# Attention heads' wide float32 products as three one-pass products of exact halves, and sums over partitions as two

## The chip, the cores and the metric

The kernel runs on one core of a Trainium2 chip. The metric is the device time of one execution in microseconds; the time before is the median of three runs. The engines are named as in the profile: PE multiplies (PEld is its weight load, which overlaps it), DVE is the vector engine, ACT the scalar (activation) engine, POOL the general one, SP the engine that issues most DMAs.

## What is computed

A two-layer decoder trunk on 256 tokens of width 2048, all in float32. Cut to the parts that the change touches:

```python
def memory_attention(q_m, mem, g_mem, w_mem_kv):        # both layers, 4 heads of 128
    s = jnp.einsum('bshd,bmhd->bhsm', q, k) * (MEM_HEAD_DIM ** -0.5)
    p = jax.nn.softmax(s, axis=-1)
    return jnp.einsum('bhsm,bmhd->bshd', p, v)

def mla_attention(...):                                 # layer 1, 12 heads, causal
    s = (einsum(q_nope, k_nope) + einsum(q_rope, k_rope)) * scale     # k_rope: one for all heads
    p = jax.nn.softmax(where(k_pos <= q_pos, s, -inf), axis=-1)
    return p @ v

def rmsnorm(x, g):
    return x * lax.rsqrt(jnp.mean(x * x, axis=-1) + EPS) * g
```

Layer 0 mixes with a gated unit beside the memory heads, layer 1 with the 12 causal heads beside the memory heads; each layer then has an output projection and a gated FFN of width 5632 with a short convolution.

## The kernel before

**Numbers.** The activations lie with features on the partitions and the 256 tokens in the columns. A large product is not done as a float32 product. Both operands are split into a high part of type fp32r (ACT copies the value to that type) and a low part, the exact rest (DVE subtracts). Then three products are added in PSUM: high by high, high by low, low by high. The big multiplications do this with weights `whi`, `wlo` and activations such as `xhl`, whose first 256 columns are the high part and whose last 256 are the low part (`mm_fm`, lines 148 to 155, and `mm_tm`, lines 181 to 186). The smaller products of the heads are plain float32 products: the memory heads' scores (line 584) and outputs (line 619), the causal heads' scores (line 956 for the plain part, line 957 for the rotary part) and outputs (lines 990 and 991), the sums over partitions by a matrix of ones (line 265), and all transposes by the identity. In the trace a plain float32 product shows as two instructions, an fp32r product as one.

**Weight stream.** `chunk` (line 95) loads a piece of weights (usually 128x1024) into `raw` (4 buffers), ACT writes `whi` (line 113; 5 buffers), DVE writes `wlo` (line 114; 5 buffers), and PE uses the two for 24 fp32r products of 256 columns, or 12 of 512. `whi` of a chunk is free again when the chunk's last product with it has run.

**Order.** The program text gives each instruction a priority. The order on every engine is fixed when the program is built, by a planner that runs a model of the engines' times (`schedule_with_timeline_sim=True`, line 1133) and gives each engine, at each moment of the model, the ready instruction that comes first in the text. On the chip every engine runs its list in that order, and an instruction that waits holds up all behind it on its engine. Dependencies and semaphores are added by the same layer. `hooks` are pieces of work that a big multiplication calls after the chunk of the given number.

**Stages.** The memory's keys `kT` and values `mv` for both layers, and the turned input `xhl`, come first (`start`). `layer_a` then does the gate's values, the memory queries `qm`, and the gate's other half in three multiplications; in the first two of these lie two memory heads each: scores after chunks 2 and 3, transposes after chunk 5, outputs after chunks 6 and 7. The spatial weights `wT` and biases `bb` are last used by `gates(9)` after chunk 0. `w_out`, `ffn`, `layer_b`, `w_out` and `ffn` follow.

**The heads of layer 1.** `layer_b` builds the latents (`latent`, with `rstd_bc`), the rotary key `krz` (line 894), the memory queries, and the values `v` (line 909) in `scratch`, which takes the place of `xhl`. Then a loop of six iterations, one for each pair of heads, does in iteration i:

- `queries(i)` and `keys(i)`: weights of three chunks, results copied by ACT into `qn` and `kn`;
- `rotary(i)`: six POOL instructions turn the pair's rotary queries into `qr`;
- `turn` of the pair before last and of a memory head: transposes of the probabilities, copied by ACT into `pT`;
- `scores` of the last pair: for each head, four products into one PSUM bank (128 and 256 keys; plain, then rotary), then mask and maximum (DVE, line 963), exponent (ACT, line 969), division (DVE, line 974);
- `attend` of the pair before last, `memory_out` of one memory head, `memory_scores` of the next.

After the loop stand `scores` of the last pair and `w_out`, which begins with the four memory heads' blocks and has the last two pairs' transposes and outputs as hooks. All of PSUM is eight banks, one tile each (`psum`).

`rstd_bc` (line 263) is called five times: for each FFN (after chunk 3 of its first multiplication), at the start of `layer_b`, and for the two latents. It multiplies the ones by `ssum`, a running sum of squares that POOL keeps (lines 271 to 275).

Of the kernel before, what the change touches and what calls it, by code (L numbers as in the profile page):

```python
# [16 lines left out]
P = 128  # L17
D = 2048
S = 256
# [50 lines left out]
class Kernel:  # L70
# [192 lines left out]
    def rstd_bc(self, out, ssum, n):  # L263
        acc = self.psum()
        self.nc.tensor.matmul(acc[:, :S], self.ones, ssum, start=True, stop=True)
        self.rstd(out, acc[:, :S], n, self.cp, "rb")
# [11 lines left out]
    def constants(self):  # L278
        nc, cp = self.nc, self.cp
        self.ident = cp.tile([P, P], F32, name="ident")  # L280
        make_identity(nc, self.ident)
        self.ones = cp.tile([P, P], F32, name="ones")
        nc.vector.memset(self.ones, 1.0)
        self.gT = cp.tile([P, 148], F32, name="gT")
        self.cT = cp.tile([P, 2, 4, FB * 2], F32, name="cT")
        self.g = {}
        self.ng = 0
# [142 lines left out]
    def start(self):  # L430
        nc, t, tc = self.nc, self.t, self.tc
        self.x = self.ap.tile([P, NB, S], F32, name="xT")
        self.xhl = self.ap.tile([P, NB, 512], F32R, tag="xhl", name=self.uid("xhl"))
# [5 lines left out]
        with tc.tile_pool(name="st", bufs=1) as st:  # L439
# [12 lines left out]
            def put_x(k, acc):  # L452
                for i in range(2):
                    self.split_gain(self.xhl[:, k + i, :], acc[:, i * S : (i + 1) * S], self.gain("g_mix", k + i))
                nc.scalar.activation(self.x[:, k : k + 2, :], acc.rearrange("p (k s) -> p k s", k=2), AF.Copy)
# [21 lines left out]
            def first_keys(evict):  # L477
# [35 lines left out]
                nc.scalar.activation(self.tmp(st, [P, 1], "warm", 1), self.ones[:, :1], AF.Copy)  # L513
# [66 lines left out]
    def memory_scores(self, l, h, q, pool):  # L580
        nc = self.nc
        acc = self.psum()
        for sb in range(2):
            nc.tensor.matmul(  # L584
                acc[:, sb * S : (sb + 1) * S], q[:, sb * P : (sb + 1) * P], self.kT[l][:, h, :], start=True, stop=True
            )
        scale = 128 ** -0.5
        a3 = acc.rearrange("p (a m) -> p a m", a=2)
        mx = self.tmp(pool, [P, 2], "mx", 4)
# [3 lines left out]
        den = self.tmp(pool, [P, 2], "den", 4)  # L593
        for sb in range(2):
            nc.scalar.activation(
                p[:, sb, :], a3[:, sb, :], AF.Exp, bias=mx[:, sb : sb + 1], scale=scale, accum_out=den[:, sb : sb + 1]
            )
        nc.vector.reciprocal(den, den)
        for sb in range(2):
            nc.vector.tensor_scalar(p[:, sb, :], p[:, sb, :], den[:, sb : sb + 1], None, ALU.mult)  # L600
        return p

    def memory_turn(self, p, pool, bufs=2):
        nc = self.nc
        acc = self.psum()
# [6 lines left out]
        nc.scalar.activation(pT, acc, AF.Copy)  # L612
        return pT

    def memory_out(self, l, h, pT, hl):
        nc, v = self.nc, self.mv[l]
        o = self.psum()
        for mb in range(2):
            nc.tensor.matmul(o[:, :S], v[:, mb, h * P : (h + 1) * P], pT[:, mb * S : (mb + 1) * S], start=mb == 0, stop=mb == 1)  # L619
        self.split(hl[:, GH + h, :], o[:, :S])  # L620
# [5 lines left out]

    def new_hl(self):
        self.xhl = self.ap.tile([P, NB, 512], F32R, tag="xhl", name=self.uid("xhl"))
        self.ssum = self.tmp(self.cp, [P, S], "ssum", 2)

    def next_operand(self, j, gain):
        x = self.x[:, j, :]
        if gain is None:
            self.split(self.xhl[:, j, :], x)
        else:
            self.split_gain(self.xhl[:, j, :], x, gain)
        self.square_add(self.ssum, x, j == 0, self.cp)
# [19 lines left out]
    def ffn(self, l, after=None, to_tokens=None, tokens=None):  # L657
# [5 lines left out]
        with self.tc.tile_pool(name=self.uid("ff"), bufs=1) as fp:  # L663
            g0 = 0
            for part, ng in enumerate(FF_GROUPS):
# [11 lines left out]
                for g in range(g0, g0 + ng):  # L677
                    gate = self.tmp(fp, [P, 4, S], "gate", 2)

                    def eg(b, acc):  # L680
                        c = conv(4 * g + b, acc)
                        nc.scalar.activation(gate[:, b, :], c, AF.Silu)

                    def ev(b, acc):
                        c = conv(FB + 4 * g + b, acc)
                        hv = self.tmp(fp, [P, S], "hv", 2)
                        nc.vector.tensor_tensor(hv, gate[:, b, :], c, ALU.mult)
                        self.split(h[:, 4 * (g - g0) + b, :], hv)
# [3 lines left out]
                    self.gemm_fm(self.rows(up, g * 512, 512), ks, 4, lambda k: xhl[:, k, :], eg, hooks=first if g == 0 else {})  # L692
                    self.gemm_fm(self.rows(up, FF + g * 512, 512), ks, 4, lambda k: xhl[:, k, :], ev, hooks=turns)
# [21 lines left out]
    def layer_a(self):  # L715
        nc, t, tc = self.nc, self.t, self.tc
        w, xhl, rt, rb = t["w_in_a"][0], self.xhl, self.rt, self.rb
        x = lambda k: xhl[:, k, :]
        ks = list(range(NB))
        with ExitStack() as ctx:  # L720
# [5 lines left out]
            wT = la.tile([P, GH, P], F32, name="wT")  # L726
            bb = la.tile([P, GH, P], F32, name="bb")
# [52 lines left out]
            p = {}  # L780

            def scores(h):
                p[h] = self.memory_scores(0, h, qm[:, h, :], la)
# [4 lines left out]
            for c in range(3):  # L788
# [11 lines left out]
                if c < 2:  # L800
                    h = 2 * c
                    hooks = {
                        0: [lambda: gates(9)] if c == 0 else [],
                        2: [lambda h=h: scores(h)],
                        3: [lambda h=h: scores(h + 1)],
                        5: [lambda h=h: turn(h), lambda h=h: turn(h + 1)],
                        6: [lambda h=h: self.memory_out(0, h, p[h], hl)],
                        7: [lambda h=h: self.memory_out(0, h + 1, p[h + 1], hl)],
# [5 lines left out]
    def layer_b(self):  # L814
# [7 lines left out]
        x = lambda k: xhl[:, k, :]  # L822
        mm, tt = nc.tensor.matmul, nc.vector.tensor_tensor
        with tc.tile_pool(name="lb", bufs=1) as lb:
# [4 lines left out]
            krz = lb.tile([P, 2, S], F32, name="krz")  # L829
            nc.gpsimd.memset(krz, 0.0)  # L830
            qm = lb.tile([P, MH, S], F32, name="qm1")
            lt = ctx.enter_context(tc.tile_pool(name="lt", bufs=1))

# [28 lines left out]
            def rotate(dst, a):  # L862
# [6 lines left out]
                nc.gpsimd.tensor_tensor(dst, m, n, ALU.subtract)  # L869
# [14 lines left out]
            def rotate_key():  # L884
# [7 lines left out]
                for j in range(2):  # L892
                    r = slice(j * ROPE, (j + 1) * ROPE)
                    nc.gpsimd.tensor_tensor(krz[r, j, :], m[r, :], n[r, :], ALU.add)
# [8 lines left out]
            scratch = self.ap.tile([P, NB * 512], F32, tag="xhl", name="scratch")  # L903
            v = scratch[:, : 2 * GW].rearrange("p (a c) -> p a c", a=2)
            wuv = t["w_uv"][0].rearrange("r h v -> r (h v)")

            def values(c):
                def ev(tb, acc):
                    nc.scalar.activation(v[:, tb, c * 512 : (c + 1) * 512], acc, AF.Copy)
# [13 lines left out]
            def queries(pr):  # L923
# [9 lines left out]
                qn[pr] = self.tmp(lp, [P, 3, S], "qn", 2)  # L933
# [3 lines left out]
            def keys(pr):  # L937
                kn[pr] = self.tmp(lp, [P, 2, S], "kn", 2)
# [6 lines left out]
            def rotary(pr):  # L945
                qr[pr] = self.tmp(lp, [P, S], "qr", 2)
                rotate(qr[pr], qn[pr][:, 2, :])

            def scores(h):
                pr, j = divmod(h, 2)  # L950
                sc = self.psum()
                for qb in range(2):
                    n = P * (qb + 1)
                    o = sc[:, qb * P : qb * P + n]
                    q = slice(qb * P, (qb + 1) * P)
                    mm(o, qn[pr][:, j, q], kn[pr][:, j, :n], start=True, stop=False)  # L956
                    mm(o, qr[pr][:, q], krz[:, j, :n], start=False, stop=True)  # L957
                mx = self.tmp(lp, [P, 2], "mx", 4)
                den = self.tmp(lp, [P, 2], "den", 4)
                p = self.tmp(lp, [P, 3 * P], "p", 3)  # L960
                part = (slice(0, P), slice(P, 3 * P))
                for qb in range(2):
                    nc.vector.tensor_tensor_reduce(
                        out=p[:, part[qb]], in0=sc[:, part[qb]], in1=self.mask[:, (1 - qb) * P :], scale=1.0, scalar=-3.0e38,
# [12 lines left out]
            def turn(h):  # L977
# [4 lines left out]
                pT = self.tmp(lp, [P, 512], "pT", 3)  # L982
                nc.scalar.activation(pT[:, : 3 * P], acc[:, : 3 * P], AF.Copy)
                pa[h] = pT

            def attend(h):
                pT = pa.pop(h)
                o = self.psum()
                cols = slice(h * P, (h + 1) * P)
                mm(o[:, :S], v[:, 0, cols], pT[:, :S], start=True, stop=False)  # L990
                mm(o[:, P:S], v[:, 1, cols], pT[:, S : S + P], start=False, stop=True)
                self.split(hl[:, h, :], o[:, :S])

            def mscores(h):
                pm[h] = self.memory_scores(1, h, qm[:, h, :], lp)

            def mturn(h):
                pm[h] = self.memory_turn(pm[h], lp, 3)

            def mout(h):  # L1000
                self.memory_out(1, h, pm.pop(h), hl)
# [4 lines left out]
            for i in range(n):  # L1006
                queries(i)
# [7 lines left out]
                if i >= 1:  # L1015
                    scores(2 * i - 2)
                    scores(2 * i - 1)
# [6 lines left out]
            scores(2 * n - 2)  # L1024
            scores(2 * n - 1)
# [111 lines left out]
```

## Time and profile before

| | |
|---|---|
| median of three runs | 2063.09 us (2063.08 to 2063.68) |
| the profiled execution | 2063.35 us |
| its span, first to last instruction | 2061.6 us |
| granted PE clock | 0.999 |
| PE busy | 2051.8 us |
| DVE, ACT, POOL busy | 1375.7, 1075.2, 141.0 us |
| DMA moved | 392.55 MB, 190 GB/s |

A row of the timeline has the start, the length, the engine, the line, the operation, output and inputs, the tile's form and the number of equal instructions merged. A PE row's length is modelled to the end of the result and overlaps the next row, so the price of a product is read from one start to the next. In a row of groups the numbers after the bar are the busy time, the mean of one instruction in ns, the idle time before them on their engine and what ended it.

### The profile page before, as it was taken

Reading aid. Unit: us, or ns where it says so; the run is one execution under the profiler, and the core shown is the slowest. Engines: PE = TensorE matmul, PEld = TensorE weight load, DVE = VectorE, ACT = ScalarE, POOL = GpSimd, SP = SyncE. Lnnn points to the kernel's source line nnn. Section 1 sums busy time; section 2 is a strip of 40 time slices with the busy share of each in tenths; the row PEclk is TensorE's granted clock in tenths of the full one; section 3 lists DMA queues with packets and bytes.
Section 4 is the critical chain, followed back from the end, with each engine's and each line's share of the span. In section 5 each row is a group of like instructions: output and inputs, shape, how many; then the busy total and the mean of one; then the engine's idle time right before and its main releaser. Section 6 shows DMA issues by size and latency. Waiting matters only on the chain.

```text
span 2061.6 us, 39720 instructions
## 1 busy us (share of the span) xinstructions
PE 2051.8 (100%) x16316; PEld 1982.9 (96%) x16316; DVE 1375.7 (67%) x2051; ACT 1075.2 (52%) x1537; POOL 141.0 (7%) x200
## 2 busy tenths in 40 slices
PE   9999999999999999999999999999999999999998
PEld 8989999999999999999999999999988999889996
DVE  6656666777656767557788676776765677646765
ACT  7754644555434555345555574455543555435554
POOL 0000013100000000000042241400000000000000
PEclk9999999999999999999999999999999999999999
DMA  8665455666556665566655634565655666556653
GB/s 288 197 216 176 154 194 197 193 195 195 194 195 195 194 194 192 195 194 192 197 191 178 185 119 169 183 202 184 192 191 193 196 197 194 189 194 195 196 183 143
DMA packets 207690, 392.55 MB, mean 190 GB/s; under 512 B 14158, under 2 KB 23188, under 8 KB 207380
## 3 DMA queue, kind: packets, MB, share of 16 engines
q1 hardware_dynamic: 207316, 389.48, 58.5%
q8 instruction: 127, 2.08, 0.4%
q10 hardware_dynamic: 192, 0.54, 0.1%
q14 instruction: 55, 0.45, 0.1%
HBM read 387.88 MB, written 2.10 MB: 189 GB/s over the span
## 4 chain that ended last, share of the span: by engine, by line
PE 99%; ACT 0%; DMA 0%; DVE 0%; issue 0%; ACTq 0%
PE ps L152 26%; PE ps L153 26%; PE ps L155 26%; PE ps L185 6%; PE ps L184 6%; PE ps L186 6%; PE ps L507 1%; PE ps L956 0%; PE ps L957 0%; PE ps L400 0%; PE ps L619 0%; PE ps L584 0%; PE ps L767 0%; PE ps L990 0%; PE ps L981 0%; PE ps L608 0%
## 5 line engine op out<-in xcount | busy, mean ns | idle before, releaser
L114 DVE TENSOR_TENSOR wlo<-raw,whi 128x1024 fp32r<-128x1024 f32 x660 | 818.0, 1242 | 544.1 <-ACT whi L113 537.8
L113 ACT ACTIVATE whi<-raw 128x1024 fp32r<-128x1024 f32 x660 | 700.8, 1062 | 868.6 <-PE ps L153 661.9
L152 PE MATMUL ps<-xhl,whi 128*128 128x256 f32 x3264 | 764.6, 277 | 0.0
L153 PE MATMUL ps<-xhl,whi 128*128 128x256 f32 x3264 | 761.1, 276 | 0.0
L153 PEld LDWEIGHTS ps<-xhl,whi 128*128 128x128 f32 x3264 | 612.7, 188 | 0.5
L152 PEld LDWEIGHTS ps<-xhl,whi 128*128 128x128 f32 x3264 | 612.7, 188 | 0.5
L155 PE MATMUL ps<-xhl,wlo 128*128 128x256 f32 x3264 | 437.1, 276 | 0.0
L155 PEld LDWEIGHTS ps<-xhl,wlo 128*128 128x128 f32 x3264 | 400.6, 188 | 0.0
L152 PE MATMUL ps<-h,whi 128*128 128x256 f32 x704 | 163.6, 276 | 0.0
L153 PE MATMUL ps<-h,whi 128*128 128x256 f32 x704 | 163.6, 276 | 0.0
L185 PE MATMUL ps<-wlo,h 128*128 128x512 f32 x354 | 137.3, 388 | 0.0
L184 PE MATMUL ps<-whi,h 128*128 128x512 f32 x354 | 137.3, 388 | 0.0
L186 PE MATMUL ps<-whi,h 128*128 128x512 f32 x354 | 137.0, 388 | 0.0
L153 PEld LDWEIGHTS ps<-h,whi 128*128 128x128 f32 x704 | 131.9, 188 | 0.0
L152 PEld LDWEIGHTS ps<-h,whi 128*128 128x128 f32 x704 | 131.8, 188 | 0.0
L152 PE MATMUL ps<-mainhl,whi 128*128 128x256 f32 x512 | 119.7, 277 | 0.0
L153 PE MATMUL ps<-mainhl,whi 128*128 128x256 f32 x512 | 119.5, 276 | 0.0
L672 ACT ACTIVATE c<-a,cT 128x256 f32<-128x256 f32 x176 | 99.4, 588 | 0.0
L153 PEld LDWEIGHTS ps<-mainhl,whi 128*128 128x128 f32 x512 | 96.1, 188 | 0.0
L152 PEld LDWEIGHTS ps<-mainhl,whi 128*128 128x128 f32 x512 | 96.1, 188 | 0.0
L155 PE MATMUL ps<-h,wlo 128*128 128x256 f32 x704 | 94.1, 276 | 0.0
L232 DVE TENSOR_TENSOR a<-ps,rbc 128x256 f32<-128x256 f32 x176 | 69.9, 418 | 27.7 <-PE ps L155 27.7
(273 smaller groups left out, 2196.0 us busy)
## 6 DMA issues: line engine op xcount, KB each, us to landing
raw<-in_w_ffn_up SPq DMA_DIRECT2D x352, 512.0 KB, 3.5
raw<-in_w_ffn_down SPq DMA_DIRECT2D x176, 512.0 KB, 4.3
raw<-in_w_out SPq DMA_DIRECT2D x64, 512.0 KB, 4.4
raw<-in_w_in_a SPq DMA_DIRECT2D x56, 512.0 KB, 3.9
raw<-in_w_mem_kv SPq DMA_DIRECT2D x31, 512.0 KB, 4.6
raw<-in_w_in_b SPq DMA_DIRECT2D x16, 512.0 KB, 4.0
raw<-in_w_kv_a SPq DMA_DIRECT2D x9, 512.0 KB, 4.0
raw<-in_w_uq SPq DMA_DIRECT2D x12, 384.0 KB, 3.2
```

The lines of the kernel that those rows point to most:

```text
L113: nc.scalar.activation(hi[:, :n], raw[:, :n], AF.Copy)
L114: nc.vector.tensor_tensor(lo[:, :n], raw[:, :n], hi[:, :n].bitcast(F32), ALU.subtract)
L152: mm(acc[:, :S], wh, x[:, :S], start=first, stop=False)
L153: mm(acc[:, :S], wh, x[:, S:], start=False, stop=False)
L155: mm(acc[:, :S], wl, x[:, :S], start=False, stop=last)
L184: mm(acc, xh, wh, start=first, stop=False)
L185: mm(acc, xh, wl, start=False, stop=False)
L186: mm(acc, xl, wh, start=False, stop=last)
L232: self.nc.vector.tensor_tensor(out, acc[:, :S], r, ALU.mult)
L507: nc.tensor.matmul(acc[:, :S], w[:, o : o + P], x, start=k == 0 and n == 0, stop=k == NB - 1 and n == 2)
L672: nc.scalar.activation(c, a, AF.Identity, scale=w(2), bias=w(3))
```

## The change

- **Memory heads** (both layers). A new function `memory_split` writes the halves of a head's keys, queries and values. The scores become three fp32r products for each of the two query blocks, the outputs three for each of the two blocks of memory tokens. The transposed probabilities get a high part (ACT) and a low part (DVE). In `layer_a` the splits of a pair of heads are called after chunk 1, and their tiles (`slots`) take the place of `wT` and `bb`; in `layer_b` one head's splits are called at the start of iterations 1 to 4.
- **Causal heads.** `rotate` now ends in a split of the rotary queries (ACT, DVE), and the rotary key is split once. The rotary scores of a pair come first in the bank: three fp32r products per query block with the keys of both heads side by side (256 and 512 columns). The plain scores are added after them as plain float32 products. A bank holds one query block of two heads, where it held two query blocks of one head. The outputs' product with the first 128 keys (256 columns) becomes three fp32r products; the one with the last 128 keys (128 columns) stays a float32 product.
- **Sums by ones.** `rstd_bc` splits `ssum` (ACT, DVE) and multiplies an fp32r matrix of ones by the two parts.
- **Room.** `whi` has 4 buffers in place of 5. `xhl` is two tiles of eight blocks each; in `layer_b` one of them holds `v1`, `qn` and `kn`, the other the values' halves and the memory keys' halves.

The diff, cut to its core:

```diff
     def split_tile(self, tag, moves=False):
-        w = self.wp.tile([P, 1088], F32R, tag=tag, name=self.uid(tag), bufs=5)
+        w = self.wp.tile([P, 1088], F32R, tag=tag, name=self.uid(tag), bufs=4 if tag == "whi" else 5)
...
     def rstd_bc(self, out, ssum, n):
         acc = self.psum()
-        self.nc.tensor.matmul(acc[:, :S], self.ones, ssum, start=True, stop=True)
+        parts = [self.tmp(self.cp, [P, S], "sq", 2).bitcast(F32R) for _ in range(2)]
+        self.nc.scalar.activation(parts[0], ssum, AF.Copy)
+        self.nc.vector.tensor_tensor(parts[1], ssum, parts[0].bitcast(F32), ALU.subtract)
+        for i, part in enumerate(parts):
+            self.nc.tensor.matmul(acc[:, :S], self.ones1, part, start=i == 0, stop=i == 1)
...
+    def three(self, o, w, x, start, stop):
+        mm, (wh, wl), (xh, xl) = self.nc.tensor.matmul, w, x
+        mm(o, wh, xh, start=start, stop=False)
+        mm(o, wh, xl, start=False, stop=False)
+        mm(o, wl, xh, start=False, stop=stop)
+
+    def memory_split(self, l, h, q, keys, rest):
+        i, v = h % 2, self.mv[l][:, :, h * P : (h + 1) * P]
+        k, q2, v2 = (a[:, o + i * 512 : o + (i + 1) * 512] for a, o in ((keys, 0), (rest, 0), (rest, 1024 + (24, 32)[l])))
+        self.split(k, self.kT[l][:, h, :])
+        self.split(q2, q)
+        for tb in range(2):
+            c = slice(tb * P, (tb + 1) * P)
+            self.nc.scalar.activation(v2[:, c], v[:, tb, :], AF.Copy)
+            self.nc.vector.tensor_tensor(v2[:, S + tb * P : S + (tb + 1) * P], v[:, tb, :], v2[:, c].bitcast(F32), ALU.subtract)
+        return k, q2, v2
...
         for sb in range(2):
-            nc.tensor.matmul(
-                acc[:, sb * S : (sb + 1) * S], q[:, sb * P : (sb + 1) * P], self.kT[l][:, h, :], start=True, stop=True
-            )
+            c, o = slice(sb * P, (sb + 1) * P), slice(S + sb * P, S + (sb + 1) * P)
+            self.three(acc[:, sb * S : (sb + 1) * S], (q[:, c], q[:, o]), (k[:, :S], k[:, S:]), True, True)
...
-        pT = self.tmp(pool, [P, 512], "pT", bufs)
-        nc.scalar.activation(pT, acc, AF.Copy)
+        pT = self.tmp(pool, [P, 1024], "mpT", bufs, F32R)
+        nc.scalar.activation(pT[:, :512], acc, AF.Copy)
+        nc.vector.tensor_tensor(pT[:, 512:], acc, pT[:, :512].bitcast(F32), ALU.subtract)
...
-            nc.tensor.matmul(o[:, :S], v[:, mb, h * P : (h + 1) * P], pT[:, mb * S : (mb + 1) * S], start=mb == 0, stop=mb == 1)
+            c, m = (slice(mb * P, (mb + 1) * P), slice(S + mb * P, S + (mb + 1) * P)), slice(mb * S, (mb + 1) * S)
+            self.three(o[:, :S], (v[:, c[0]], v[:, c[1]]), (pT[:, m], pT[:, 512:][:, m]), mb == 0, mb == 1)
...
-                nc.gpsimd.tensor_tensor(dst, m, n, ALU.subtract)
+                nc.gpsimd.tensor_tensor(m, m, n, ALU.subtract)
+                self.split(dst, m)
...
-            def scores(h):
-                pr, j = divmod(h, 2)
-                sc = self.psum()
+            def scores(pr):
+                bank = [self.psum() for _ in range(2)]
                 for qb in range(2):
                     n = P * (qb + 1)
-                    o = sc[:, qb * P : qb * P + n]
-                    q = slice(qb * P, (qb + 1) * P)
-                    mm(o, qn[pr][:, j, q], kn[pr][:, j, :n], start=True, stop=False)
-                    mm(o, qr[pr][:, q], krz[:, j, :n], start=False, stop=True)
+                    q = [qr[pr][:, i * S + qb * P : i * S + (qb + 1) * P] for i in range(2)]
+                    both = bank[qb][:, : 2 * n].rearrange("p (j k) -> p j k", j=2)
+                    self.three(both, q, [k[:, :, :n] for k in krz], True, False)
+                    for j in range(2):
+                        mm(both[:, j, :], qn[pr][:, j, qb * P : (qb + 1) * P], kn[pr][:, j, :n], start=False, stop=j == 1)
+                for j in range(2):
+                    softmax(2 * pr + j, [bank[qb][:, j * P * (qb + 1) : (j + 1) * P * (qb + 1)] for qb in range(2)])
...
-                nc.scalar.activation(pT[:, : 3 * P], acc[:, : 3 * P], AF.Copy)
+                pT, last = self.tmp(lp, [P, 576], "pT", 2, F32R)[:, 13 : 13 + 512], self.tmp(lp, [P, P], "pl", 2)
+                self.split(pT, acc[:, :S])
+                nc.scalar.activation(last, acc[:, S : 3 * P], AF.Copy)
...
-                mm(o[:, :S], v[:, 0, cols], pT[:, :S], start=True, stop=False)
-                mm(o[:, P:S], v[:, 1, cols], pT[:, S : S + P], start=False, stop=True)
+                self.three(o[:, :S], (vh[:, cols], vl[:, cols]), (pT[:, :S], pT[:, S:]), True, False)
+                mm(o[:, P:S], v1[:, cols], last, start=False, stop=True)
```

More of the change, by code (lines that the diff above doesn't have):

```diff
@@ L625, in add_residual, with halves @@
         nc.vector.tensor_tensor(x[:, j, :], acc[:, :S], x[:, j, :], ALU.add)
+    def halves(self):
+        tiles = [self.ap.tile([P, NB // 2, 512], F32R, tag=f"xhl{i}", name=self.uid("xhl")) for i in range(2)]
+        return [tiles[k // (NB // 2)][:, k % (NB // 2), :] for k in range(NB)]
     def new_hl(self):
-        self.xhl = self.ap.tile([P, NB, 512], F32R, tag="xhl", name=self.uid("xhl"))
+        self.xhl = self.halves()
         self.ssum = self.tmp(self.cp, [P, S], "ssum", 2)
@@ L633, in next_operand @@
         if gain is None:
-            self.split(self.xhl[:, j, :], x)
+            self.split(self.xhl[j], x)
         else:
-            self.split_gain(self.xhl[:, j, :], x, gain)
+            self.split_gain(self.xhl[j], x, gain)
         self.square_add(self.ssum, x, j == 0, self.cp)
```

101 lines of the change are left out of this document (61 added, 40 removed).

## The prediction

> **What bounds the kernel now.** I read the head of the page first, then its chain of work that ended last and its groups, then PE's timeline.
>
> ```profile
> span 2061.6 us, 39720 instructions
> PE 2051.8 (100%) x16316; PEld 1982.9 (96%) x16316; DVE 1375.7 (67%) x2051; ACT 1075.2 (52%) x1537; POOL 141.0 (7%) x200
> ...
> PE 99%; ACT 0%; DMA 0%; DVE 0%; issue 0%; ACTq 0%
> ...
> L113 ACT ACTIVATE whi<-raw 128x1024 fp32r<-128x1024 f32 x660 | 700.8, 1062 | 868.6 <-PE ps L153 661.9
> ```
>
> PE is busy for all but 10 of 2062 us, and the chain is 99% PE. ACT, which makes the weights' high parts, mostly waits for PE to give a buffer back (661.9 of the 868.6 us that it idles before them). So the time is the sum of what PE's products cost, and a cheaper product shortens the kernel by what it saves, as long as its operands come in time. Two questions follow: what PE saves, and whether the added work of ACT and DVE ever makes PE wait.
>
> **What PE saves.** Prices are read from start to start. First the one-pass products, and a memory head in `layer_a`:
>
> ```profile
> 181.96 1.07 PE L155 MATMUL ps<-xhl,wlo 128*128 128x256 f32 x8
> 184.68 0.50 PE L155 MATMUL ps<-xhl,wlo 128*128 128x256 f32 x3
> ...
> 206.48 1.07 PE L155 MATMUL ps<-xhl,wlo 128*128 128x256 f32 x8
> 207.39 1.03 PE L584 MATMUL ps<-kT,qm 128*128 128x256 f32 x4
> 210.08 1.07 PE L155 MATMUL ps<-xhl,wlo 128*128 128x256 f32 x8
> ```
>
> A chunk of 24 products of 256 columns lies between 181.96 and 184.68: 2.72 us, or 0.113 each. Between 206.48 and 210.08 lie one chunk and the two score products of a head (four instructions): 3.60 - 2.72 = 0.88, or 0.44 for a float32 product of 256 columns in a group that stands between one-pass products. Three one-pass products cost 0.34: 0.10 less.
>
> Products of 512 columns, from the values' stage, with 71 intervals between these two rows:
>
> ```profile
> 1150.14 0.40 PE L184 MATMUL ps<-whi,chl 128*128 128x512 f32 x1
> ...
> 1166.26 0.39 PE L186 MATMUL ps<-whi,chl 128*128 128x512 f32 x1
> ```
>
> 16.12 / 71 = 0.227 each. Now one iteration of the loop over the pairs of heads:
>
> ```profile
> 1217.60 0.81 PE L981 MATMUL ps<-ident,p 128*128 128x128 f32 x6
> ...
> 1218.91 0.39 PE L957 MATMUL ps<-krz,qr 128*128 128x128 f32 x2
> 1219.13 0.60 PE L956 MATMUL ps<-kn,qn 128*128 128x256 f32 x2
> 1219.57 0.59 PE L957 MATMUL ps<-krz,qr 128*128 128x256 f32 x2
> 1220.00 0.38 PE L956 MATMUL ps<-kn,qn 128*128 128x128 f32 x2
> ...
> 1221.31 0.59 PE L990 MATMUL ps<-pT,scratch 128*128 128x256 f32 x2
> 1221.74 0.38 PE L991 MATMUL ps<-pT,scratch 128*128 128x128 f32 x2
> ...
> 1222.62 1.03 PE L619 MATMUL ps<-pT,mv 128*128 128x256 f32 x4
> 1223.48 1.03 PE L584 MATMUL ps<-kT,qm 128*128 128x256 f32 x4
> ```
>
> Among other float32 products, one of 256 columns costs 0.43 (1219.57 to 1220.00, 1221.31 to 1221.74), one of 128 columns 0.22 (1218.91 to 1219.13), and two of 256 cost 0.86 (1222.62 to 1223.48). The 0.88 above is that plus 0.02, the price of one change to the other kind and back. The terms:
>
> - Memory heads: 8 heads with 2 score and 2 output products each. In `layer_a` 16 x (0.44 - 0.34) = 1.6, in `layer_b` 16 x (0.43 - 0.34) = 1.4; together 3.0 us.
> - Causal outputs: 12 x (0.43 - 0.34) = 1.1 us. The products of 128 columns stay.
> - Rotary scores of a pair: before 2 x (0.22 + 0.43) = 1.30, after 3 x 0.113 + 3 x 0.227 = 1.02. Six pairs save 1.7 us. The plain scores stay.
> - Sums by ones: five, 0.44 before and 2 x 0.113 after: 1.1 us.
> - Changes of kind: transposes, rotary scores, plain scores, outputs and last keys now alternate, about 3 more changes in each of 6 iterations: 18 x 0.02 = 0.4 us lost (between 0 and 0.4; I take the 0.4).
>
> Sum: 6.9 - 0.4 = **6.5 us saved on PE**.
>
> **What is added beside PE.** The nearest rows for the new splits, and the load of two iterations of the loop (the columns after the length are PE, PEld, DVE, ACT, POOL):
>
> ```profile
> L241 DVE TENSOR_TENSOR mainhl<-ps,mainhl 128x256 fp32r<-128x256 f32 x20 | 8.0, 416 | 0.0
> L241 DVE TENSOR_TENSOR xhl<-xT,xhl 128x256 fp32r<-128x256 f32 x16 | 13.6, 902 | 0.0
> L450 DVE TENSOR_TENSOR memhl<-ps,memhl 128x512 fp32r<-128x512 f32 x8 | 5.5, 691 | 7.6 <-ACT memhl L449 7.6
> L240 ACT ACTIVATE mainhl<-ps 128x256 fp32r<-128x256 f32 x20 | 7.1, 371 | 2.9 <-PE ps L991 1.6 <-PE ps L619 1.3
> ```
>
> ```profile
> 1197.00:1210.50 13.50, 13.50 (x103) 13.01 (x102) 9.94 (x31) 9.53 (x30) 5.08 (x6) 1.00 0.36 118
> 1210.50:1224.10 13.60, 13.60 (x103) 13.08 (x103) 9.21 (x27) 9.25 (x26) 5.46 (x6) 1.00 0.36 118
> ```
>
> In an iteration with a memory head DVE gains subtractions for the keys, the queries, the values and the rotary queries (4 x 0.42, the values' two halves taken as one) and for the transposed probabilities (2 x 0.42 + 0.69): 3.2 on top of 9.2 to 9.9, so 12.4 to 13.1. ACT gains some 6 x 0.37 = 2.2 on top of 9.4. PE's iteration shrinks from 13.6 by 0.28 (rotary), 0.18 (two outputs) and 0.36 (a memory head), and grows by 0.06: 12.8. So DVE is as good as full in four iterations. What hides this is that the weight splits, three chunks' worth in each iteration, are far ahead and can slip:
>
> ```profile
> 1214.24 2.48 DVE L114 TENSOR_TENSOR wlo<-raw,whi 128x1024 fp32r<-128x1024 f32 x2
> ...
> 1242.24 0.52 PE L155 MATMUL ps<-mainhl,wlo 128*128 128x256 f32 x3
> ```
>
> The second of these two splits ends at 1216.72 and is first used at 1242.24, 25 us later. What cannot slip is the way from the transposes to the outputs:
>
> ```profile
> 1218.43 0.87 ACT L983 ACTIVATE pT<-ps 128x384 f32<-128x384 f32 x2
> 1219.17 0.62 ACT L612 ACTIVATE pT<-ps 128x512 f32<-128x512 f32 x1
> ```
>
> From 1218.43 ACT now has four copies (0.37 each) and the memory head's (0.62), to 1220.5; DVE's low part of that takes 0.69, to 1221.2. PE needs it for the memory output, at 1222.62 - 0.28 - 0.18 = 1222.2. The causal outputs (1221.31 - 0.28 = 1221.0) need a low part that is done at about 1220. So 1.0 us is left, less than one weight split (1.24) that happens to stand in front on DVE. I take 0.6 us of such waits over the loop (between 0 and 0.8 in each of four iterations, the first rival).
>
> At the loop's end stands the one place where the rotary queries are wanted at once:
>
> ```profile
> 1235.22 0.72 POOL L869 TENSOR_TENSOR qr<-rm,rn 128x256 f32<-128x256 f32 x1
> 1237.50 0.39 PE L957 MATMUL ps<-krz,qr 128*128 128x128 f32 x2
> ```
>
> POOL ends at 1235.94, 1.56 before PE's use. Now ACT and DVE follow (0.37 and 0.42 at least), so the low part is there at 1236.7. PE arrives 0.6 earlier, and the rotary products now precede the plain ones (another 0.44): 1236.4, with the low part as third product 0.2 later. I take 0.4 us of wait (between 0 and 0.9), since the output projection's first blocks are memory heads and might be put in front.
>
> The sums by ones now wait for ACT and DVE after POOL:
>
> ```profile
> 365.67 2.60 POOL L275 TENSOR_TENSOR ssum<-ssum,sq 128x256 f32<-128x256 f32 x2
> ...
> 371.31 0.59 PE L265 MATMUL ps<-ssum,ones 128*128 128x256 f32 x2
> ```
>
> POOL ends 3.0 us before PE. Copy and subtraction take 0.8 and may each stand behind one weight split (1.06 and 1.24): 3.1, so nothing, or 0.1.
>
> One `whi` buffer less brings each weight split one chunk, 2.72 us, nearer to its use. The closest that I found after the first 60 us is in the gate's values:
>
> ```profile
> 131.06 1.23 DVE L114 TENSOR_TENSOR wlo<-raw,whi 128x1024 fp32r<-128x1024 f32 x1 [3.36 <-ACT whi L113]
> ...
> 137.60 0.39 PE L185 MATMUL ps<-wlo,xhl 128*128 128x512 f32 x1
> ```
>
> It ends at 132.29, 5.3 before its use; 2.6 would remain. I cost it at nothing. If that cover were gone as well, PE would wait at that place by what is missing. The splits in `layer_a` (two heads, some 2.5 us of DVE after chunk 1) come out of the same lead: nothing.
>
> **Sum.** 2063.35 (the profiled execution) - 6.5 + 0.6 + 0.4 = 2057.85. That execution was 0.26 above the median of the three runs, so I predict **2057.6 us**.
>
> **The rivals.**
>
> *DVE keeps the loop's old period.* If the four iterations with a memory head stay at 13.6 us, because a low part stands behind a weight split on DVE, 4 x 0.8 = 3.2 us are lost: 2060.8. For it speaks DVE's 12.4 to 13.1 against 12.8, against it the 25 us by which weight splits can slip.
>
> *DVE becomes the loop's bound (slower).* The same subtraction of 128x256 took 416 ns from PSUM and 902 ns with both inputs in SBUF, in a stage where POOL squares the same tiles. In the loop POOL works 5.1 to 5.5 of 13.6 us. If the four subtractions with both inputs in SBUF take 902, DVE needs up to 13.1 + 1.9 = 15.0; if each also waits for a POOL instruction of 0.72 (the row of L869), 17 or so. Then four iterations grow by 2.2 to 4.2: 9 to 17 us, 2066 to 2074, in the middle 2070. From 14.2 us per iteration on it eats all of the gain, from some 15.2 on the kernel is slower. Against it: POOL is busy for only 40% of the loop, and the weight splits can slip into the projection after it.
>
> The Trainium skill, "SBUF — State Buffer", section "Who interferes with whom", says that a DVE instruction with two SBUF inputs and a POOL instruction that reads SBUF exclude each other for a whole instruction. The rows of 902 and 416 agree that there is a price, though the 902 is about twice and not a wait of many. By the rule taken to its end the time would be this rival's upper one.
>
> *The side-by-side keys are not one pass.* All one-pass products in the trace have 256 or 512 columns in one piece. If two pieces of 128 columns cost like two float32 products of 0.22, the first query block takes 1.32 in place of 0.34: six pairs lose 5.9, 2063.5.
>
> **How the numbers follow.** A measurement of this kernel can tell about 0.2% (4.1 us) from no change, so faster means below 2059.0 and slower above 2067.2. The forecast (up to 2.4 us of waits in all) gets 0.65, the old period 0.17, the pieces 0.03, DVE as the bound 0.15, of which 0.03 fall short of slower. So faster 0.65, same 0.23, slower 0.12. The range begins where no wait and no change of kind costs anything (2063.09 - 6.9 = 2056.2) and reaches over the old period with its 0.9 at the loop's end: 2056.0 to 2062.0. It leaves out 0.18.
>
> **What would show it.** In the changed profile PE's products at the scores' and outputs' lines show as one-pass ones, a memory head's scores at 0.68 where 0.88 stood, a pair's rotary scores at 1.02. The loop's period says which case holds: about 12.8, 13.6, or over 14.2. A wait of PE for `pT`'s or the memory heads' low part, or a late weight split in the loop, shows the two DVE rivals; a wait at the sums or in the gate's values would make the two zeros above wrong.

## The result and the profile after

The changed kernel takes 2110.85 us (median of 6 runs, 2110.29 to 2112.32), the kernel before 2063.39 us beside it (6 runs): 1.0231 times as long, 95% interval 1.0218 to 1.0244. The prediction said 2057.6. The head of the changed kernel's page, its chain by engine, and two groups:

```profile
span 2109.7 us, 39907 instructions
PE 2096.2 (99%) x16348; PEld 2028.6 (96%) x16348; DVE 1401.3 (66%) x2118; ACT 1088.2 (52%) x1593; POOL 142.4 (7%) x200
...
PE 98%; POOL 1%; ACT 0%; DVE 0%; DMA 0%; issue 0%; ACTq 0%; POOLq 0%
...
L113 ACT ACTIVATE whi<-raw 128x1024 fp32r<-128x1024 f32 x660 | 700.0, 1061 | 903.3 <-PE ps L153 673.6
L152 PE MATMUL ps<-xhl,whi 128*128 128x256 f32 x3264 | 784.1, 280 | 0.0
```

Of the 48.1 us by which the span grew, 44.4 are PE's busy time (2051.8 before); PE's idle time grew from 9.8 to 13.5, by 3.7. So waits are a small part of it. PE has 32 instructions more, yet it is busier, and a group that the change doesn't touch has become dearer: `L152`, the weights' products, has the same 3264 instructions in both. Here is its row before, from the page:

```profile
L152 PE MATMUL ps<-xhl,whi 128*128 128x256 f32 x3264 | 764.6, 277 | 0.0
```

A row's length overlaps the next, so it hides most of the difference. The number of products in a fixed stretch shows it. In both kernels 400 to 1100 us is one-pass products of 256 columns without a gap, nearly all of them FFN 0's (before, the sum by ones at 1089.85 us lies among them). First before, then after, the view by stretches (stretch, length, busy time and count of PE, PEld, DVE, ACT, POOL, granted clock, DMA share, GB/s):

```profile
400.00:1100.00 700.00, 700.00 (x6177) 699.95 (x6176) 475.60 (x679) 351.58 (x455) 29.22 (x32) 1.00 0.61 194
```

```profile
400.00:1100.00 700.00, 700.00 (x5836) 700.00 (x5835) 443.96 (x632) 328.49 (x419) 14.43 (x15) 1.00 0.57 183
```

700 / 6177 = 113.3 ns for a product before, 700 / 5836 = 120.0 ns after. PE counts as 100% busy in both and the granted clock is 1.00 in both: neither column shows it. So PE has two paces for the same product. Where does it change? PE's timeline of the changed kernel around the first sum by ones, in FFN 0:

```profile
369.36 0.96 PE L155 MATMUL ps<-xhl,wlo 128*128 128x256 f32 x7
370.15 0.41 PE L269 MATMUL ps<-sq,ones 128*128 128x256 f32 x2
370.39 0.28 PE L152 MATMUL ps<-xhl,whi 128*128 128x256 f32 x1
370.51 0.28 PE L153 MATMUL ps<-xhl,whi 128*128 128x256 f32 x1
370.63 0.28 PE L152 MATMUL ps<-xhl,whi 128*128 128x256 f32 x1
370.75 0.28 PE L153 MATMUL ps<-xhl,whi 128*128 128x256 f32 x1
...
1189.98 1.02 PE L925 MATMUL ps<-kr,both 128*128 128x256 f32 x4
...
1191.56 0.28 PE L152 MATMUL ps<-xhl,whi 128*128 128x256 f32 x1
1191.67 0.28 PE L153 MATMUL ps<-xhl,whi 128*128 128x256 f32 x1
1191.78 0.28 PE L152 MATMUL ps<-xhl,whi 128*128 128x256 f32 x1
1191.89 0.28 PE L153 MATMUL ps<-xhl,whi 128*128 128x256 f32 x1
...
1386.16 0.40 PE L269 MATMUL ps<-sq,ones 128*128 128x256 f32 x2
```

Seven products before the pair of `L269` take 0.79 (0.113 each); the pair and all behind it go at 0.12. That lasts 821 us, until the rotary key's plain float32 products (`L925`); from 1191.56 on it is 0.11 again. Three more pairs lie in this stretch (1130.71, 1156.87 and 1183.99), and PE is at 0.12 behind each of them too. FFN 1's pair at 1386.16 does the same for 72 us, until the plain transposes of the output (`L1114`, from 1458.40). The two slow stretches hold 6843 and 613 PE instructions (counts of the view by stretches), and 7456 x 6.7 ns = 50 us. That is the whole result, to within the small gains and waits below.

### The profile page after: what moved, and what is told of

Same layout as the page of the kernel before. It is cut to its first block, busy times and chain, and to the rows that moved or that the text cites. A ratio compares the mean times of both kernels' runs of the same rounds, so it can differ in the third digit from the quotient of the medians.

```text
span 2109.7 us, 39907 instructions
## 1 busy us (share of the span) xinstructions
PE 2096.2 (99%) x16348; PEld 2028.6 (96%) x16348; DVE 1401.3 (66%) x2118; ACT 1088.2 (52%) x1593; POOL 142.4 (7%) x200
## 4 chain that ended last, share of the span: by engine, by line
PE 98%; POOL 1%; ACT 0%; DVE 0%; DMA 0%; issue 0%; ACTq 0%; POOLq 0%
PE ps L153 26%; PE ps L152 26%; PE ps L155 26%; PE ps L185 6%; PE ps L184 6%; PE ps L186 6%; PE ps L512 1%; POOL rn L905 0%; PE ps L405 0%; PE ps L587 0%; PE ps L588 0%; PE ps L589 0%; PE ps L795 0%; PE ps L1002 0%; PE ps L1114 0%; DMA graw<-in_g_mem 0%
## 5 line engine op out<-in xcount | busy, mean ns | idle before, releaser
L152 PE MATMUL ps<-xhl,whi 128*128 128x256 f32 x3264 | 784.1, 280 | 0.0
L153 PE MATMUL ps<-xhl,whi 128*128 128x256 f32 x3264 | 783.0, 280 | 0.0
L152 PEld LDWEIGHTS ps<-xhl,whi 128*128 128x128 f32 x3264 | 613.2, 188 | 0.1
L155 PE MATMUL ps<-xhl,wlo 128*128 128x256 f32 x3264 | 448.4, 280 | 0.0
L155 PEld LDWEIGHTS ps<-xhl,wlo 128*128 128x128 f32 x3264 | 410.8, 188 | 0.0
L152 PE MATMUL ps<-h,whi 128*128 128x256 f32 x704 | 172.3, 283 | 0.0
L153 PE MATMUL ps<-h,whi 128*128 128x256 f32 x704 | 172.3, 283 | 0.0
L152 PEld LDWEIGHTS ps<-h,whi 128*128 128x128 f32 x704 | 132.1, 188 | 0.0
L152 PE MATMUL ps<-mainhl,whi 128*128 128x256 f32 x512 | 119.7, 277 | 0.0
L155 PE MATMUL ps<-h,wlo 128*128 128x256 f32 x704 | 98.8, 283 | 0.0
L152 PEld LDWEIGHTS ps<-mainhl,whi 128*128 128x128 f32 x512 | 96.1, 188 | 0.0
```

Of the source, the lines that this page charges most:

```text
L152: mm(acc[:, :S], wh, x[:, :S], start=first, stop=False)
L153: mm(acc[:, :S], wh, x[:, S:], start=False, stop=False)
L155: mm(acc[:, :S], wl, x[:, :S], start=False, stop=last)
```

## The experiments

**The sums, undone and alone.** My theory after the trace: the pair of one-pass sums starts the slow pace and a float32 product ends it. The rival: something else in the changed kernel (tiles moved in memory, the split tiles' addresses) makes the weights' products slower. `e1_undo_sums` is the changed kernel with

```diff
-        for i, part in enumerate(parts):
-            self.nc.tensor.matmul(acc[:, :S], self.ones1, part, start=i == 0, stop=i == 1)
+        self.nc.tensor.matmul(acc[:, :S], self.ones, ssum, start=True, stop=True)
```

`e2_sums_alone` is the kernel before with the changed `rstd_bc` and `ones1`, and nothing else. `e3_reset` is the changed kernel with a float32 product of 64 columns of zeros, added to the sum, behind each pair:

```diff
+        self.nc.tensor.matmul(acc[:, :64], self.ones, self.mask[:, :64], start=False, stop=True)
```

> The changed kernel with one part undone: the five sums by ones are plain float32 products of the unsplit sums again; all else stays. Theory A: in the changed kernel's trace PE's products of 256 columns take 120 ns from the first FFN's sum (370 us) to the rotary key (1191 us) and again from the second FFN's sum (1386 us) to the final transposes (1460 us), and 113 ns elsewhere; the one-pass sums put PE into the slower pace, and only a float32 product takes it out. 894 us at 120 in place of 113 are 50 us too many, so this kernel should take 2110.9 - 50 + 1 = 2062 us, with 113 ns throughout. Rival B: the pace comes from the new places in SBUF (whi with 4 buffers, xhl in two tiles), and the start at the sum is chance: this kernel stays at about 2111.

> The kernel before with one part of the change alone: the one-pass sums. Theory A: PE falls to 120 ns at the first FFN's sum (about 371 us) and stays there to the rotary key (1147 us before), and again from 1341 to 1410: 845 us, 47 us longer, about 2109. Rival B: 113 ns throughout, about 2062.

> The changed kernel with one small plain float32 product (ones by 64 columns of zeros, added into the same sum) after each pair of one-pass products of the sums. Theory A, in the form that a float32 product takes PE back to 113 ns: 2110.9 - 50 + 5 x 0.13 = 2061.5. If what keeps PE slow is only the two waits for ACT and DVE at the sums, a float32 product behind them changes nothing: about 2111. Rival B: about 2111.

Measured: e1 2063.86 us, 1.0003 times before (0.9994 to 1.0012); e2 2111.95 (one run, before 2062.83); e3 2062.75, 1.0000 (0.9991 to 1.0010). All three are 1 to 3 us above what the theory said for them, against 47 us in question. The view by stretches of e1, e2 and e3, in this order:

```profile
400.00:1100.00 700.00, 700.00 (x6176) 699.95 (x6176) 476.47 (x681) 351.60 (x455) 30.09 (x33) 1.00 0.65 194
```

```profile
400.00:1100.00 700.00, 700.00 (x5836) 700.00 (x5835) 443.81 (x631) 328.80 (x420) 14.94 (x16) 1.00 0.61 183
```

```profile
400.00:1100.00 700.00, 700.00 (x6179) 700.00 (x6178) 476.44 (x681) 352.10 (x457) 29.69 (x32) 1.00 0.65 194
```

The sums alone bring all of the loss, without them it is gone, and a float32 product behind them takes it away again. (Whether any added product would do so, a one-pass one too, was not tried.) PE's timeline of e3 shows the cure at work (`L270` is the added product):

```profile
369.56 0.40 PE L269 MATMUL ps<-sq,ones 128*128 128x256 f32 x2
369.80 0.33 PE L270 MATMUL ps<-mask,ones 128*128 128x64 f32 x2
...
370.62 0.28 PE L153 MATMUL ps<-xhl,whi 128*128 128x256 f32 x1
370.74 0.28 PE L152 MATMUL ps<-xhl,whi 128*128 128x256 f32 x1
370.85 0.28 PE L153 MATMUL ps<-xhl,whi 128*128 128x256 f32 x1
370.96 0.28 PE L152 MATMUL ps<-xhl,whi 128*128 128x256 f32 x1
371.08 0.28 PE L153 MATMUL ps<-xhl,whi 128*128 128x256 f32 x1
371.19 0.28 PE L152 MATMUL ps<-xhl,whi 128*128 128x256 f32 x1
```

After the float32 product the weights' products need 0.12 for six or so, then 0.11 to 0.115: PE settles back. The product costs 0.14 us (369.80 to 369.94). The rival falls.

**Why this pair and no other one-pass product?** The memory heads' products are one-pass too and stand in the same stream, but no such stretch follows them. In each of them at least one operand starts at an odd column of its tile (13 or 19 in most), and the weights' parts start 19 columns in; the sums' three operands (the ones, the high and the low part) all start at column 0. So I moved starts, by columns of 4 bytes. `e4_parts_offset` and its kin:

```diff
-        parts = [self.tmp(self.cp, [P, S], "sq", 2).bitcast(F32R) for _ in range(2)]
+        parts = [self.tmp(self.cp, [P, 288], "sq", 2)[:, 19 : 19 + S].bitcast(F32R) for _ in range(2)]
```

(the squares of `square_add` use the first 256 columns of the same tiles), with both parts 16 columns in for `e6_parts_16`, both 8 in for `e11_parts_8`, the first (high) part alone 19 in for `e7_first_part`, the second (low) part alone 19 in for `e12_second_part`. `e5_ones_offset` leaves the parts and moves the ones:

```diff
-        self.ones1 = cp.tile([P, P], F32R, name="ones1")
+        self.ones1 = cp.tile([P, P + 32], F32R, name="ones1")[:, 19 : 19 + P]
```

> The changed kernel with the two parts of each sum 19 columns further in their tiles, at another address modulo 64 and 128 bytes, as other operands of the kernel have it. Theory A without a role of the address: 120 ns in the same stretches, about 2111. Theory A with the address of the moving operand as what decides which pace PE falls into: 113 ns throughout, about 2061.

> The changed kernel with the matrix of ones 19 columns further in its tile, the parts of the sums where the change put them. If only the address of the moving operand (the parts) decides which pace PE falls into, 120 ns in the same stretches and about 2111. If the address of the weights of the last product before the stream decides as well, 113 ns and about 2063.

> As the run with the parts 19 columns (76 bytes) further, but by 16 columns (64 bytes). If the address modulo 64 bytes is what counts, PE falls to 120 ns again, about 2111. If the address modulo 128 bytes or more, 113 ns and about 2063.

> As the run with both parts 19 columns further, but with the first (high) part alone moved; the second (low) part, the last operand that PE reads before the weights' products go on, stays at the tile's beginning. If the last product before the stream sets the pace: 120 ns, about 2111. If the first one or any one of the two does: 113 ns, about 2063.

> The counterpart of the run with the first part alone moved: the second (low) part of each sum 19 columns further, the first at the tile's beginning. If one odd address among ones and parts is enough, wherever it is: 113 ns throughout and about 2062. If it has to be the ones or the first part: 120 ns and about 2110.

> As the run with both parts 19 columns further, but by 8 columns (32 bytes). If PE falls to the slower pace whenever the parts begin at a multiple of 32 bytes: about 2110, 120 ns from at least one of the FFNs' sums on. If 64 bytes is the step that matters: 113 ns throughout and about 2062.

| one run each | moved | us (before) | pace after the FFNs' sums |
|---|---|---|---|
| e4 | both parts by 19 | 2063.22 (2062.83) | 113 ns |
| e5 | ones by 19 | 2062.22 (2062.86) | 113 ns |
| e7 | high part by 19 | 2061.09 (2062.86) | 113 ns |
| e12 | low part by 19 | 2062.70 (2064.11) | 113 ns |
| e6 | both parts by 16 | 2109.48 (2062.86) | 120 ns |
| e11 | both parts by 8 | 2063.70 (2064.11) | 113 ns |

So at the FFNs' sums the starts of the operands decide: one of the three 19 columns further is enough, a move of both parts by 64 bytes leaves the loss. (The wider tile alone doesn't do it, since e6 has it too; e5 makes the tile of the ones 128 bytes wider, which may move others too.) The move by 32 bytes fits neither side of what I had expected: after the FFNs' sums PE stayed at 113 ns, but it ran at 120 from the sum at the start of `layer_b` to the first latent's (1088.5 to 1115.1) and from the second latent's to the rotary key (1140.3 to 1147.6). And e6 shows that a pair doesn't always slow PE down. Its sum for the first latent found PE at 120 ns and left it at 113 (timeline of e6):

```profile
1129.46 1.12 PE L155 MATMUL ps<-xhl,wlo 128*128 128x256 f32 x8
1130.42 0.40 PE L269 MATMUL ps<-sq,ones 128*128 128x256 f32 x2
...
1131.37 0.28 PE L152 MATMUL ps<-xhl,whi 128*128 128x256 f32 x1
1131.48 0.28 PE L153 MATMUL ps<-xhl,whi 128*128 128x256 f32 x1
1131.59 0.28 PE L152 MATMUL ps<-xhl,whi 128*128 128x256 f32 x1
```

Eight products take 0.96 before it (0.12 each), and 0.11 to 0.12 behind it. My reading of all this, which is argued and not shown: each product of another kind in the stream settles the pace anew, to one of two values that then hold; the pair at those starts settles it at 120 in an FFN. The start alone can't be the rule, since in e6 and in e11 the same starts gave both paces at different sums. What the rule is, and what in PE keeps the pace, stays open.

Single runs differ by some 2 us before the pace comes into play: the first product of the gates comes at 188.31 us before and anywhere from 187.4 to 189.3 in the runs. Counted from there to the end of the span, the traces agree closely: 1873.3 before, 1871.8 to 1872.0 in e4, e5, e7 and e12, 1921.35 in the changed kernel. The slow pace thus costs 49.5 us, against the 50 from counting products. e11 has 1873.7, and its two stretches at 120 ns hold some 280 products, 1.9 us.

**The waits.** Even at 113 ns throughout, e1, e3 and e4 are where the kernel before is, not 5.5 us below it. The views of waits and of the timeline of the changed kernel show the loss in the loop over the pairs. Who waited for whom (us in total, times, longest), 1200 to 1290 us:

```profile
ACT qr L240 <- POOL rm L906: 12.5, 5, 2.8
DVE qr L241 <- ACT qr L240: 6.1, 4, 1.9
...
PE ps L587 <- ACT qr L240: 2.5, 2, 1.3
```

and the first of PE's two waits, on all engines:

```profile
1223.69 0.72 POOL L906 TENSOR_TENSOR rm<-rm,rn 128x256 f32<-128x256 f32 x1
1224.45 0.42 ACT L240 ACTIVATE qr<-rm 128x256 fp32r<-128x256 f32 x1 [2.21 <-POOL rm L906]
...
1224.90 0.60 DVE L241 TENSOR_TENSOR qr<-rm,qr 128x256 fp32r<-128x256 f32 x1 [1.87 <-ACT qr L240]
1224.92 0.19 PEld L587 LDWEIGHTS ps<-krz,qr 128*128 128x128 f32 x1 [1.40 <-ACT qr L240]
...
1224.92 0.38 PE L587 MATMUL ps<-krz,qr 128*128 128x256 f32 x1 [1.20 <-ACT qr L240]
```

ACT reaches the split of the rotary queries 2.2 us too early and stands there, since POOL has not finished the rotation; DVE stands behind ACT; and all that they would have done for PE in that time is late as well. From start to start, beyond the products' own prices, PE loses 1.36 us here, 0.72 at a transpose at 1235.94 that waits for `p`, 0.81 at the first output of the pair (`pT`'s low part, 1239), and 1.40 at the loop's end, where POOL finishes at 1281.22 and PE goes on at 1281.72: 4.3 us. Two kernels test this, both on e4. `e8_rotary_plain` gives the rotary scores back to plain float32 behind the plain ones, so that nothing is split behind POOL:

```diff
-                nc.gpsimd.tensor_tensor(m, m, n, ALU.subtract)
-                self.split(dst, m)
+                nc.gpsimd.tensor_tensor(dst, m, n, ALU.subtract)
...
-                    self.three(both, q, [k[:, :, :n] for k in krz], True, False)
                     for j in range(2):
-                        mm(both[:, j, :], qn[pr][:, j, qb * P : (qb + 1) * P], kn[pr][:, j, :n], start=False, stop=j == 1)
+                        mm(both[:, j, :], qn[pr][:, j, q], kn[pr][:, j, :n], start=True, stop=False)
+                        mm(both[:, j, :], qr[pr][:, q], kr[:, j, :n], start=False, stop=True)
```

`e9_plain_first` keeps the one-pass rotary scores, but puts the plain scores ahead of them in the bank:

```diff
-                    self.three(both, q, [k[:, :, :n] for k in krz], True, False)
                     for j in range(2):
-                        mm(both[:, j, :], qn[pr][:, j, qb * P : (qb + 1) * P], kn[pr][:, j, :n], start=False, stop=j == 1)
+                        mm(both[:, j, :], qn[pr][:, j, qb * P : (qb + 1) * P], kn[pr][:, j, :n], start=j == 0, stop=False)
+                    self.three(both, q, [k[:, :, :n] for k in krz], False, True)
```

> The kernel with the sums' parts 19 columns further (113 ns throughout), and the rotary scores undone: plain float32 products after the plain scores, no split of the rotary queries and keys. In the kernel with the split PE waits four times in the loop (1.4, 0.7, 0.8 and 1.4 us), and ACT and DVE stand still in front of the split until POOL has turned the queries. If the split behind POOL is what makes all four waits, they go, and the rotary products cost 1.7 more: about 2063.0 - 4.2 + 1.7 = 2060.5. If the waits for p and pT come from the new low halves of pT or from DVE's load, two of the four stay: about 2062.

> The kernel with the sums' parts 19 columns further, and the plain scores put before the rotary ones in each bank. The rotary operands are then wanted up to 0.9 us later. If the split behind POOL makes the waits, those at the loop's start and end shrink by about 0.6 each: about 2061.8. If the order of the products does not matter, about 2063.0, with the same four waits.

Measured: e8 2058.51 us, 0.9979 times before (0.9970 to 0.9988); e9 2061.28, 0.9991 (0.9982 to 1.0000). The heads of the two pages, e8 first:

```profile
span 2057.1 us, 39919 instructions
...
PE 2047.2 (100%) x16360; PEld 1980.9 (96%) x16360; DVE 1395.5 (68%) x2111; ACT 1086.1 (53%) x1586; POOL 142.3 (7%) x200
```

```profile
span 2059.4 us, 39907 instructions
...
PE 2047.0 (99%) x16348; PEld 1978.7 (96%) x16348; DVE 1398.9 (68%) x2118; ACT 1088.1 (53%) x1593; POOL 142.9 (7%) x200
```

Their busy times are the same, and the 2.3 us between the spans are idle time of PE. (A row's length runs over the start of a wait: of the 1.36 us at 1224.92, 1.20 count as idle. So busy time isn't the price of the products: an iteration of the loop takes 13.09 us in e8 and 12.84 to 12.88 in e4.) In e8 the view of waits shows no wait of PE in the loop at all, `p` and `pT` included: all four places hang on the rotary split. In e9 the products that went ahead cover a part of it, and what is left shows up a step later:

```profile
PE ps L1030 <- DVE p L1023: 2.0, 4, 1.0
```

e8 is faster than both kernels, by 0.2% of the kernel before, and 2.0 us below the 2060.5 that I had expected. Part of that is the start again: from the rotary key's products to the end of the span the traces have 915.0 us before, 915.7 in e4, 912.5 in e8 and 915.4 in e9. So e8 gains 3.2 there, where 4.2 - 1.7 = 2.5 was expected, and e9 gains 0.3 where 1.2 was expected. Doing the rotary split on POOL itself was not tried.

**The buffers.** `e10_whi4` is the kernel before with four `whi` buffers in place of five:

```diff
-        w = self.wp.tile([P, 1088], F32R, tag=tag, name=self.uid(tag), bufs=5)
+        w = self.wp.tile([P, 1088], F32R, tag=tag, name=self.uid(tag), bufs=4 if tag == "whi" else 5)
```

> The kernel before with one part of the change alone: 4 buffers for whi in place of 5. The prediction costed it at nothing: within 0.1% of the kernel before, no wait of PE for a weight split after the first 60 us. The rival that the lead is needed: waits of PE at group ends, some 0.5 us in each of 30 groups, 2078.

Measured: 2063.63 us, 1.0002 times before (0.9993 to 1.0012).

## Why the prediction was wrong

**The step that failed** stands at the head of its argument: "the time is the sum of what PE's products cost, and a cheaper product shortens the kernel by what it saves". The 0.113 of a one-pass product was read once, at 181.96 us, and taken as a price that holds for all of the weights' products. It is one of two paces, and the pairs of the sums, which themselves were to save 1.1 us in all, set some 7,400 others to the dearer one. What a new product does to the price of those behind it was put at nothing, without a reason; it cost 50 us. No rival held this: two were about DVE, the third about the price of the side-by-side keys themselves. The trace of before had a sign of it. Its chain of work that ended last has, in the loop, right behind plain transposes that stand between weights' products:

```profile
1241.68 0.12 PE ps L152
1241.80 0.12 PE ps L153
...
1242.40 0.96 PE ps L155 x8
...
1245.28 0.95 PE ps L155 x8
```

beside 0.91 for the same eight in FFN 0 (`400.94 0.91 PE ps L155 x8` in that view). A second price for the same form was there to be read, and it asked what sets it. It also shows that a float32 product doesn't always bring the faster pace: here it is two float32 transposes that the 0.12 follows.

The other steps, with the pace out of the way (e1, e3, e4):

- **The sums by ones**, 1.1 us: right as a price. Before against e4, each of the five places is 0.2 us shorter, 1.0 together (from the sum to the 14th or 15th product behind it).
- **The memory heads**, 1.6 us in `layer_a`: 1.2 in e4 (183.0 us from the gates' first product to the first sum before, 181.8 in e4). Among themselves the new products cost 0.118, not 0.113: three 0.354.
- **The loop's period**: right. The transposes of two iterations begin at 1249.24, 1262.09 and 1274.96, so 12.85 and 12.87 against the 12.8 forecast. The view by stretches of the changed kernel:

```profile
1249.24:1262.09 12.85, 12.85 (x109) 12.61 (x108) 11.86 (x36) 10.31 (x36) 5.06 (x6) 1.00 0.39 127
1262.09:1274.96 12.87, 12.87 (x109) 12.63 (x107) 10.17 (x32) 9.60 (x29) 5.61 (x6) 1.00 0.36 119
```

- **DVE as the bound**: no. It has 10.2 to 11.9 of 12.9 us. Nor did the doubled price come: the groups by shape, 1190 to 1290 us, have the splits with both inputs in SBUF at 456 and 553 ns, where POOL is busy 40% of the time. The Trainium skill, "SBUF — State Buffer", section "Who interferes with whom", would have such a split wait out a POOL instruction that reads SBUF and started first; against the 412 of a split of the same size from PSUM (`pT`), these means leave room for that in few of them.

```profile
L241 DVE TENSOR_TENSOR qr<-rm,qr 128x256 fp32r<-128x256 f32 x6 | 2.7, 456 | 6.2 <-ACT qr L240 6.1
L241 DVE TENSOR_TENSOR rest<-qm,rest 128x256 fp32r<-128x256 f32 x4 | 2.2, 553 | 0.0
```

- **The waits**, 0.6 in the loop and 0.4 at its end: 4.3 measured, a mis-sized term. The 0.4 was worked out from POOL's end before PE's use in the kernel before; what was left out is that ACT and DVE, standing in order in front of the split, hold up everything behind it, the exponents and `pT` too. The rotary part so costs 4.3 us of waits. What it saves on PE, forecast at 1.7, is nearer 1.4: 0.23 for each of six iterations (13.09 in e8, 12.86 in e4). So e8, without it, gains.
- **`whi` with four buffers**: nothing, as forecast (e10). **The side-by-side keys** are one pass: the 256 columns at 1224.92 are one instruction, not two.

Without the slow pace, with these prices (0.4 less from the heads, 0.3 from the rotary scores, 0.1 from the sums) and with the measured waits, the sum would have been 6.5 - 0.8 - 4.3 = 1.4 us faster. Counted from the gates' first product to the end of the span, e4 is 1.3 faster than the kernel before. As times of whole runs, e4, e5, e7 and e12 lie between 0.4 above and 1.8 below it, and e3, with its added products of 0.7 us in all, at 1.0000 (0.9991 to 1.0010).

## What to carry to other kernels

Read the price of the commonest product in several stages and count products in a fixed stretch: a busy share of 100% at full clock hides two paces, 6% apart. When a product in a dense stream is replaced, look at the products behind it, not only at its own length, and if they have slowed, try another start address for its operands or a small float32 product after it; both helped here, but neither is shown to help everywhere. Before a split is put behind a slow engine's chain, ask what else stands behind it on the engines that do the split.

## What the runs showed of the hardware

- A one-pass product of 256 columns goes at 113.3 or at 120.0 ns in a steady stream, at the same granted clock (0.999); the slower pace held for 821 us, across three more pairs of the sums. The Trainium skill, "TensorE: Matmul & The Clock Gate", section "Wait — 56ns, not 53.3ns?", has for products back to back the columns at 2.4 GHz and 2.5 ns more, an estimate of 109.2 ns for 256; neither pace agrees, and it has no second one.
- A pair of one-pass products whose three operands start at column 0 of their tiles, or whose parts start 64 bytes in, set the slower pace in an FFN; one of its operands 76 bytes further (one run each), or a float32 product of 64 columns behind it (0.14 us), avoided it. At other sums the same starts gave both paces (e6, e11), and before the change two float32 transposes are followed by the slower one too (0.12, from 1241.08 to 1246.24).
- ACT stood 12.5 us, in five waits, in front of a split whose input POOL had not finished, and DVE 6.1 us, in four waits, behind ACT. PE's waits that went with the split (e8) came to 4.3 us.
